# A QKV projection whose start-up is rearranged: one block cut finer, one weight load held back, two products moved forward

## The chip, the cores and the metric

The kernel runs on one core of one Trainium2 chip. Its time is that of one execution on the device in microseconds (us); several executions are taken and their median counts. The core has five engines that each work through their own queue: TensorE (PE, with its weight loads shown apart as PEld), VectorE (DVE), ScalarE (ACT), GpSimd (POOL) and SyncE (SP). In this kernel SP does nothing but issue transfers; ACT and POOL issue a few as well. All transfers of a core share 16 DMA engines.

## The reference, cut to what matters

```
x:     (16, 512, 768)  float32
w_qkv: (768, 2304)     float32

qkv = np.matmul(x, w_qkv)
q, k, v = qkv[..., :768], qkv[..., 768:1536], qkv[..., 1536:]
return np.stack([q, k, v], axis=0).astype(np.float32)
```

It is one product of an 8192 x 768 matrix with a 768 x 2304 matrix, written out as three matrices of 8192 x 768.

## The kernel before, in words

**Tiling.** The 8192 rows are 32 pairs of two 128-row tiles (a pair `p` has rows `r` = 0 and 1). The contraction of 768 is `KT` = 6 slices of 128, in two halves of `KH` = 3 (slices j = 0 to 2 and j = 3 to 5). The 2304 columns are four blocks of 512 (`CB`) in two groups `q` = 0 and 1, each with column blocks `c` = 0 and 1, and 256 remaining columns (`REM`) between the groups.

**Two ways to multiply.** From the third pair (`p` = 2) on, each pair is multiplied with each group `q` by a Strassen-Winograd scheme: a "quad" of 2 x 2 output blocks from seven products of 128 x 384 by 384 x 512 instead of eight (`do(u, 1)` to `do(u, 7)`). Products 1 and 2 take the rounded bf16 rows `xb` and bf16 weights `b1`. The other five take sums of row quarters `sr` (`sums_x`) and sums of weight quarters `ts` (`sum_w`), in f32r. The remaining 256 columns are multiplied plainly in bf16 (`rem`). Pairs 0 and 1 are multiplied wholly in plain bf16 (`block`, `rems_by_halves`), because the sums of the weights do not exist yet while the weights are still arriving.

**The start, where the change lies.** The program's order is written by hand, and each engine keeps that order. SP loads the rows of pairs 0 and 1, then the twelve slices of the weights of group 0 (`load_slices(0, ...)` for column block 0 and `load_slices(1, ...)` for column block 1, one slice j per transfer, the first in two parts), then the rows of pair 2 in eight parts (`load_x_rows(2)`: four for row tile 0, four for row tile 1), then the weights of group 1, column block 0, in two loads (`load_blocks(1, 0)`), and later column block 1 likewise. POOL loads the 256 remaining columns in two K halves, `w_rem[0]` and `w_rem[1]`, 128 x 768 values each, cast to bf16 on the way (L435). It first runs `hold` (L428): a copy of one column that makes POOL wait until a given tile has landed. Before the change it waits once, for slice 5 of column block 0, and issues both halves. A second `hold` waits for the first rows of pair 2; behind it on POOL stands the copy `b22` (L541), one of the operands of product 3.

TensorE's order in that stretch is: block (0, 0) of pairs 0 and 1 (four output tiles, one slice after the other); block (0, 1) of the same tiles; the remaining columns of pairs 0 and 1, first K half for both pairs and then second K half (`rems_by_halves`, L321); products 1 and 2 of pair 2 with group 0 (`do(u, 1)`, `do(u, 2)`); the remaining columns of pair 2 (`rem(2)`, L575); products 5 and 6 (`middle`, L576); then block (1, 0) slice by slice, with products 7, 3 and 4 of pair 2 between its slices (`rest`, `end`).

Block (0, 1) is ordered by groups of slices and tiles: slices 0, 1 and 2 each over all four tiles, and then, tile by tile, slices 3, 4 and 5 together:

```
late = block(
    0, 1, bt, [((j, ), range(4)) for j in range(KH)] + [(range(KH, KT), range(4))]
)
```

A slice of column block 1 must be cast to bf16 (into `bt`) before it is used: slices 0 to 3 on DVE (L450), slices 4 and 5 on ACT (L448). DVE also makes the weight sums (`sum_w`, L120; `sum_w(0, 2)` needs slices 3 to 5 of column block 1) and turns the rows of pair 2 (`transpose(2, 2)`, L154, one instruction for each row tile). ACT rounds the turned rows to bf16, one instruction for each row tile (`round_row`, L200), and copies finished tiles out of the accumulators (`late[n]`, L462; the remaining columns L316; product 1 L253). `do(u, 2)` ends with an addition on DVE that adds product 2 to product 1 (L266).

The accumulators are eight banks used in turn. At this point four belong to block (0, 1), two to the remaining columns of pairs 0 and 1, and two to products 1 and 2 of pair 2. SP's stores of the remaining columns (L317) stand in its queue behind `load_blocks(1, 1)` and ahead of the loads of pair 3 (`load_x_rows(3)`).

Of the kernel before, what the change touches and what calls it, by code (L numbers as in the profile page):

```python
# [10 lines left out]
def kernel(  # L11
# [20 lines left out]
    nc = tc.nc  # L32
# [6 lines left out]
    KT = K // P  # L39
    KH = KT // 2  # L40
    KC = K // 4
    NP = M // (2 * P)
    CB = 512
# [7 lines left out]
    add = mybir.AluOpType.add  # L51
# [34 lines left out]
    bt = both[:, 1].bitcast(bf16).rearrange("p (j n) -> p j n", j=KT)  # L86
# [8 lines left out]
    stage = {}  # L95
# [7 lines left out]
    def load_blocks(q, c):  # L103
        for h in range(2):
            if c == 0 and h == 0:
                t = st_first
            else:
                t = st_pool.tile([P, KH, CB], fp32, name="st1", tag="st")[:]
            load_w(t, h * KH, KH, Q_OFF[q] + c * CB, CB)
            stage[q, h, c] = t  # L110

    def sum_w(q, n):
        t1, t2, t3, t4 = ts[q]
        o, in0, in1 = {
            1: (t1, stage[q, 0, 1], stage[q, 0, 0]),
            2: (t2, stage[q, 1, 1], t1),
            3: (t3, stage[q, 1, 1], stage[q, 0, 1]),
            4: (t4, stage[q, 1, 0], t2),
        }[n]
        nc.vector.tensor_tensor(o, in0, in1, op=sub)  # L120
# [27 lines left out]
    def transpose(p, parts=1):  # L148
        t = xf_pool.tile([P, KT, 2 * P], fp32, name="xf")
        turned = t[:].rearrange("p j (g b) -> p g j b", b=G)  # L150
        rows = xin.pop(p)[:].rearrange("p g (a j) -> p g j a", a=G)
        n = 2 * P // G // parts
        for g in range(0, 2 * P // G, n):
            nc.vector.transpose(turned[:, g:g + n], rows[:, g:g + n])  # L154
        xf[p] = t
# [39 lines left out]
    def round_row(p, r, eng):  # L195
        n = slice(r * P, (r + 1) * P)
        if r == 0:
            xb[p] = xb_pool.tile([P, KT, 2 * P], bf16, name="xb", tag="xb")
        if eng is act:
            eng.activation(xb[p][:, :, n], xf[p][:, :, n], ident)  # L200
        else:
            eng.tensor_copy(out=xb[p][:, :, n], in_=xf[p][:, :, n])
# [23 lines left out]
    def quad(p, q, pool=o_pool, tag="o"):  # L226
        u = Quad()
        u.p, u.q = p, q
        u.o = pool.tile([P, 2, 2 * CB], fp32, name="o", tag=tag)
        u.x = u.y = u.z = None  # L230
        return u

    def product(u, n, ps, start):
        t1, t2, t3, t4 = ts[u.q]
        if n <= 2:
            h = (n - 1) * KH
            lhs = [xb[u.p][:, h + j, :P] for j in range(KH)]
            rhs = [b1[u.q][:, h + j, :] for j in range(KH)]
        else:
            k, t = {3: (4, b22[u.q][:]), 4: (0, t4), 5: (1, t1), 6: (2, t2), 7: (3, t3)}[n]  # L240
            lhs = [sr[u.p][:, k, j, :] for j in range(KH)]
            rhs = [t[:, j, :] for j in range(KH)]
        for j in range(KH):
            nc.tensor.matmul(  # L244
                ps[:], lhs[j], rhs[j],
                start=(start and j == 0), stop=(j == KH - 1), skip_group_check=True,
            )

    def bank():
        return ps_pool.tile([P, CB], fp32, name="ps")  # L250

    def evacuate(u):
        nc.scalar.activation(u.o[:, 0, :CB], u.x[:], ident)  # L253

    def do(u, n, out=True):
        c11, c12 = u.o[:, 0, :CB], u.o[:, 0, CB:]
        c21, c22 = u.o[:, 1, :CB], u.o[:, 1, CB:]
        if n == 1:
            u.x = bank()
            product(u, 1, u.x, True)  # L260
            if out:
                evacuate(u)
        elif n == 2:
            u.z = bank()
            product(u, 2, u.z, True)
            nc.vector.tensor_tensor(c11, c11, u.z[:], op=add)  # L266
        elif n == 6:
            product(u, 6, u.x, False)
            nc.scalar.activation(c12, u.x[:], ident)  # L269
        elif n == 5:  # L270
            u.y = bank()
            product(u, 5, u.y, True)
        elif n == 7:
            product(u, 7, u.x, False)
            nc.scalar.activation(c22, u.x[:], ident)  # L275
            nc.vector.tensor_tensor(c22, c22, u.y[:], op=add)  # L276
        elif n == 4:
            product(u, 4, u.x, False)
            nc.scalar.activation(c21, u.x[:], ident)  # L279
        elif n == 3:  # L280
            product(u, 3, u.y, False)
            nc.vector.tensor_tensor(c12, c12, u.y[:], op=add)  # L282

    def rows_of(s, p, lo, hi):
        return out_flat[s, p * 2 * P:(p + 1) * 2 * P, lo:hi].rearrange("(r m) n -> m r n", m=P)
# [26 lines left out]
    def rem_copied(p, ps, eng=nc.sync):  # L312

        def copied():
            o = or_pool.tile([P, 2, REM], fp32, name="orem")
            act.activation(o[:], ps[:], ident)  # L316
            return lambda: eng.dma_start(rows_of(1, p, R_OFF - H, R_OFF - H + REM), o[:])  # L317

        return copied

    def rems_by_halves(pairs):  # L321
        banks = [ps_pool.tile([P, 2, REM], fp32, name="ps") for _ in pairs]
        for h in range(2):
            for p, ps in zip(pairs, banks):
                for r in range(2):
                    for j in range(KH):
                        nc.tensor.matmul(  # L327
                            ps[:, r, :], xb[p][:, h * KH + j, r * P:(r + 1) * P],
                            w_rem[h][:, j, :], start=(h == 0 and r == 0 and j == 0),
                            stop=(h == 1 and j == KH - 1), skip_group_check=True,  # L330
                        )
        return [rem_copied(p, ps) for p, ps in zip(pairs, banks)]

    def two(a, b, early, u=None):

# [87 lines left out]
    half = CB // 2  # L423
# [4 lines left out]
    def hold(src):  # L428
        mark = m_pool.tile([P, 1], fp32, name="mark")
        nc.gpsimd.tensor_copy(out=mark[:], in_=src)  # L430

    hold(stage[0, 1, 0][:, KH - 1, :1])
    for h in range(2):
        rows = w_qkv.rearrange("(p j) n -> p j n", j=KT)[:, h * KH:(h + 1) * KH]
        nc.gpsimd.dma_start(w_rem[h][:], rows[:, :, R_OFF:R_OFF + REM])  # L435
    hold(xin[2][:, 0, :1])
# [8 lines left out]
    def cast_j(q, c, w, j, eng=act, n=slice(0, CB)):  # L445
        src = stage[q, j // KH, c][:, j % KH, n]
        if eng is act:
            eng.activation(w[:, j, n], src, ident)  # L448
        else:
            eng.tensor_copy(out=w[:, j, n], in_=src)  # L450
# [3 lines left out]
    def block(q, c, w, groups, between={}):  # L454

        ps = {}
        late = []

        def finish(n):
            p, r = divmod(n, 2)  # L460
            u = quads[p, q]
            act.activation(u.o[:, r, c * CB:(c + 1) * CB], ps[n][:], ident)  # L462

        for i, (js, tiles, *cols) in enumerate(groups):
            cols = cols[0] if cols else slice(0, CB)
            for n in tiles:
                p, r = divmod(n, 2)
                fresh = n not in ps
                if fresh:
                    ps[n] = bank()  # L470
                for j in js:
                    nc.tensor.matmul(  # L472
                        ps[n][:, cols], xb[p][:, j, r * P:(r + 1) * P], w[:, j, cols],
                        start=(fresh and j == 0), stop=(j == KT - 1), skip_group_check=True,
                    )
                if KT - 1 not in js:
                    continue
                if (p, q) not in quads:
                    quads[p, q] = quad(p, q)
                late.append(lambda n=n: finish(n))  # L480
            between.get(i, lambda: None)()
        return late
# [51 lines left out]
    for f in late0:  # L534
# [5 lines left out]
    sum_w(0, 2)  # L540
    nc.gpsimd.tensor_copy(out=b22[0][:], in_=stage[0, 1, 1])  # L541
    late = block(
        0, 1, bt, [((j, ), range(4)) for j in range(KH)] + [(range(KH, KT), range(4))]
    )
    rems = rems_by_halves(range(2))
    transpose(2, 2)

    late[0]()
    late[1]()
    round_row(2, 0, act)  # L550
    rem_stores = [rems[0]()]
    late[2]()
    late[3]()
    round_row(2, 1, act)
    rem_stores.append(rems[1]())
    load_blocks(1, 1)
    for store in rem_stores:
        store()
# [7 lines left out]
    sums[2](dve)  # L566
    sum_w(0, 3)
    sums[3](dve)
    sums[4](dve)

    u = quad(2, 0)
    do(u, 1)
    do(u, 2)
    cast_j(1, 0, b1[1], 0)
    rem2 = rem(2)  # L575
    middle(u, (5, 6))  # L576
# [85 lines left out]
```

## Time and profile before

| what | value |
|---|---|
| median of 3 executions | 360.31 us (359.99 to 360.98) |
| profiled execution: its own time | 361.83 us |
| profiled execution: span of its instructions | 360.0 us |
| TensorE busy | 353.4 us, 98% of the span |
| VectorE, ScalarE, GpSimd busy | 227.8, 185.6, 178.6 us |
| granted TensorE clock | 1.00 |
| data moved | 107.73 MB, 299 GB/s over the span |
| transfers of SP's queue; of POOL's queue | 82.4%; 0.8% of 16 engines' span |

The span runs from the first instruction to the last one. The profiled execution's own time lies 1.83 us above its span, and 1.52 us above the median of the executions that were only timed. Times of single instructions below are counted from the start of the span. Matmuls follow each other closely, and each is shown longer than the distance to the next: a 128 x 512 bf16 matmul is shown with 0.38 us, while ten of them in a row take 2.15 us from first start to the next group's start. So the distances between starts, not the busy time, tell how fast TensorE works.

### The profile page before, as it was taken

What the parts mean: (1) busy time and instruction counts of PE and PEld (TensorE: products, weight loads), DVE (VectorE), ACT (ScalarE), POOL (GpSimd) and SP (SyncE); (2) the same over time, 40 slices, a digit from 0 to 9 for tenths busy, and PEclk for the clock granted to TensorE, in tenths of its full rate; (3) what the DMA queues carried; (4) which work ended last, traced back from release to release, by engine and by line L of the source; (5) the groups of instructions that cost most, each with busy time, mean ns of one, the idle gap of its engine ahead of it and who ended that gap; (6) DMA issues with size and microseconds to landing.
All of it is one profiled execution on the core that took longest, in us unless ns stands there. A gap on an engine that the chain in (4) does not pass through costs nothing.

```text
span 360.0 us, 5279 instructions
## 1 busy us (share of the span) xinstructions
PE 353.4 (98%) x1780; PEld 251.2 (70%) x1780; DVE 227.8 (63%) x244; ACT 185.6 (52%) x316; POOL 178.6 (50%) x187
## 2 busy tenths in 40 slices
PE   7999999999999999999999999999999999999995
PEld 3465577777777777777777777777777777777764
DVE  2789776756566675566675566675556676556643
ACT  4469744545454545454545444455444445545443
POOL 0221676446664445664445665444665444665420
PEclk9999999999999999999999999999999999999999
DMA  7998999898998999899999899998999998989767
GB/s 271 330 356 306 332 359 394 257 321 308 275 325 300 296 275 291 280 322 301 291 283 286 284 310 308 292 283 285 288 297 315 293 294 272 296 283 322 292 238 257
DMA packets 82107, 107.73 MB, mean 299 GB/s; under 512 B 5409, under 2 KB 62241, under 8 KB 82081
## 3 DMA queue, kind: packets, MB, share of 16 engines
q1 hardware_dynamic: 66672, 96.35, 82.4%
q10 hardware_dynamic: 14608, 10.65, 8.9%
q0 software_dynamic: 800, 0.39, 0.8%
q8 instruction: 14, 0.23, 0.3%
q14 instruction: 13, 0.10, 0.1%
HBM read 32.28 MB, written 75.50 MB: 299 GB/s over the span
## 4 chain that ended last, share of the span: by engine, by line
PE 93%; DMA 5%; ACT 1%; ACTq 1%; issue 0%
PE ps L244 78%; PE ps L299 11%; PE ps L472 4%; DMA st<-in_w_qkv_dram 3%; DMA touch<-in_x_dram 1%; PE ps L327 1%; ACT o L279 0%; ACTq L370 0%; ACT orem L384 0%; ACT both L448 0%; ACTq L416 0%; ACTq L386 0%; ACTq L384 0%
## 5 line engine op out<-in xcount | busy, mean ns | idle before, releaser
L244 PE MATMUL ps<-t,s 128*128 128x512 f32 x720 | 181.1, 399 | 0.0
L244 PEld LDWEIGHTS ps<-t,s 128*128 128x128 f32 x720 | 134.9, 188 | 30.9 <-ACT o L269 0.3
L191 POOL CAST xb<-xf 128x1536 bf16<-128x1536 f32 x28 | 40.9, 1462 | 131.1 <-DVE xf L154 131.1
L276 DVE TENSOR_TENSOR o<-o,ps 128x512 f32<-128x512 f32 x58 | 39.9, 687 | 90.5 <-ACT o L275 90.5
L154 DVE STREAM_TRANSPOSE xf<-xin 128x1536 f32<-128x1536 f32 (+1 forms) x32 | 88.9, 2783 | 2.6 <-DMA xin<-in_x_dram 2.5
L244 PE MATMUL ps<-b,xb 128*128 128x512 bf16 x360 | 87.7, 380 | 0.0
L244 PEld LDWEIGHTS <-xb 128*128 128x128 bf16 x360 | 32.8, 98 | 37.3 <-issue 7.6
L269 ACT ACTIVATE o<-ps 128x512 f32<-128x512 f32 x60 | 35.9, 598 | 44.0 <-PE ps L244 41.3
L275 ACT ACTIVATE o<-ps 128x512 f32<-128x512 f32 x58 | 34.7, 598 | 44.3 <-PE ps L244 44.3
L282 DVE TENSOR_TENSOR o<-o,ps 128x512 f32<-128x512 f32 x60 | 41.2, 687 | 21.4 <-PE ps L244 20.2
L244 PE MATMUL ps<-b,s 128*128 128x512 f32 x180 | 50.4, 389 | 0.0
L253 ACT ACTIVATE o<-ps 128x512 f32<-128x512 f32 x60 | 35.8, 597 | 24.4 <-DVE o L282 20.6
L279 ACT ACTIVATE o<-ps 128x512 f32<-128x512 f32 x60 | 35.9, 598 | 24.2 <-PE ps L244 21.3
L299 PE MATMUL ps<-w_rem,xb 128*128 128x256 bf16 x360 | 44.6, 273 | 0.0
L299 PEld LDWEIGHTS <-xb 128*128 128x128 bf16 x360 | 34.9, 98 | 11.1 <-issue 1.1
L266 DVE TENSOR_TENSOR o<-o,ps 128x512 f32<-128x512 f32 x60 | 37.8, 670 | 2.0 <-ACT o L253 1.3
L244 PEld LDWEIGHTS ps<-b,s 128*128 128x128 f32 x180 | 33.8, 188 | 7.1
L212 POOL TENSOR_TENSOR s<-s,xf 128x384 fp32r<-128x384 f32 x29 | 29.4, 1014 | 2.3
L215 POOL TENSOR_TENSOR s<-xf,s 128x384 fp32r<-128x384 f32 x29 | 29.4, 1015 | 0.0
L213 POOL TENSOR_TENSOR s<-xf 128x384 fp32r<-128x384 f32 x29 | 29.4, 1013 | 0.0
L211 POOL TENSOR_TENSOR s<-xf 128x384 fp32r<-128x384 f32 x29 | 29.3, 1012 | 0.0
L316 ACT ACTIVATE orem<-ps 128x512 f32<-128x512 f32 x31 | 18.5, 597 | 20.6 <-PE ps L299 20.1
(47 smaller groups left out, 125.9 us busy)
## 6 DMA issues: line engine op xcount, KB each, us to landing
out_dram<-o SPq DMA_DIRECT2D x62, 768.0 KB, 4.9
out_dram<-o SPq DMA_DIRECT2D x65, 256.0 KB, 4.0
xin<-in_x_dram SPq DMA_DIRECT2D x62, 192.0 KB, 6.9
xin<-in_x_dram ACTq DMA_DIRECT2D x50, 192.0 KB, 4.3
out_dram<-orem SPq DMA_DIRECT2D x31, 256.0 KB, 5.9
st<-in_w_qkv_dram SPq DMA_DIRECT2D x11, 256.0 KB, 5.8
st<-in_w_qkv_dram SPq DMA_DIRECT2D x3, 768.0 KB, 8.7
xin<-in_x_dram SPq DMA_DIRECT2D x4, 384.0 KB, 5.1
```

Source lines behind the costliest of these rows:

```text
L154: nc.vector.transpose(turned[:, g:g + n], rows[:, g:g + n])
L191: nc.gpsimd.tensor_copy(out=xb[p][:], in_=xf[p][:])
L212: 2: lambda g: g.tensor_tensor(s[:, 2], s[:, 1], a11, op=sub),
L244: nc.tensor.matmul(ps[:], lhs[j], rhs[j], start=(start and j == 0), stop=(j == KH - 1), skip_group_check=True,)
L253: nc.scalar.activation(u.o[:, 0, :CB], u.x[:], ident)
L266: nc.vector.tensor_tensor(c11, c11, u.z[:], op=add)
L269: nc.scalar.activation(c12, u.x[:], ident)
L275: nc.scalar.activation(c22, u.x[:], ident)
L276: nc.vector.tensor_tensor(c22, c22, u.y[:], op=add)
L279: nc.scalar.activation(c21, u.x[:], ident)
L282: nc.vector.tensor_tensor(c12, c12, u.y[:], op=add)
L299: nc.tensor.matmul(ps, xb[p][:, j, r * P:(r + 1) * P], w_rem[j // KH][:, j % KH, :], start=(j == 0), stop=(j == KT - 1), skip_group_check= ...
```

## The change

Three things are rearranged; the number of matmuls, transfers and additions stays the same.

- **Block (0, 1) is cut further.** Slices 0 to 3 (not 0 to 2) go over all four tiles one after the other, and only slices 4 and 5 go together, tile by tile.
- **The second half of the remaining columns' weights is held back.** `hold` is called before each of the two loads: for slice 5 of column block 0 before `w_rem[0]`, and for slice 5 of column block 1 before `w_rem[1]`. On POOL's queue the second `hold` and the second load now stand ahead of the `hold` on pair 2's rows and the `b22` copy.
- **Products 1 and 2 of pair 2 go between the two K halves of the remaining columns.** `rems_by_halves` now issues the first K half and returns a function for the second one. TensorE's order becomes: block (0, 1), first half, products 1 and 2, second half, `rem(2)`. ACT's order becomes: tiles 0 and 1 of the block, row tile 0 of pair 2 rounded, tiles 2 and 3, product 1 copied out, row tile 1 rounded, then the remaining columns of pairs 0 and 1. The addition of product 2 is split off (`add_z`) and placed on DVE between `sums[3]` and `sums[4]` of pair 2.

```
--- before.py
+++ after.py
+    def add_z(u):
+        c11 = u.o[:, 0, :CB]
+        nc.vector.tensor_tensor(c11, c11, u.z[:], op=add)
+
...
             product(u, 2, u.z, True)
-            nc.vector.tensor_tensor(c11, c11, u.z[:], op=add)
+            if out:
+                add_z(u)
...
     def rems_by_halves(pairs):
         banks = [ps_pool.tile([P, 2, REM], fp32, name="ps") for _ in pairs]
-        for h in range(2):
+
+        def half(h):
             for p, ps in zip(pairs, banks):
                 for r in range(2):
                     for j in range(KH):
...
-        return [rem_copied(p, ps) for p, ps in zip(pairs, banks)]
+
+        half(0)
+        return lambda: half(1), [rem_copied(p, ps) for p, ps in zip(pairs, banks)]
...
-    hold(stage[0, 1, 0][:, KH - 1, :1])
     for h in range(2):
+        hold(stage[0, 1, h][:, KH - 1, :1])
         rows = w_qkv.rearrange("(p j) n -> p j n", j=KT)[:, h * KH:(h + 1) * KH]
         nc.gpsimd.dma_start(w_rem[h][:], rows[:, :, R_OFF:R_OFF + REM])
     hold(xin[2][:, 0, :1])
...
     late = block(
-        0, 1, bt, [((j, ), range(4)) for j in range(KH)] + [(range(KH, KT), range(4))]
+        0, 1, bt,
+        [((j, ), range(4)) for j in range(KH + 1)] + [(range(KH + 1, KT), range(4))],
     )
-    rems = rems_by_halves(range(2))
+    second_half, rems = rems_by_halves(range(2))
     transpose(2, 2)
 
     late[0]()
     late[1]()
     round_row(2, 0, act)
-    rem_stores = [rems[0]()]
     late[2]()
     late[3]()
+    u = quad(2, 0)
+    do(u, 1)
+    do(u, 2, False)
     round_row(2, 1, act)
-    rem_stores.append(rems[1]())
+    second_half()
+    rem_stores = [r() for r in rems]
     load_blocks(1, 1)
     for store in rem_stores:
         store()
...
     sum_w(0, 3)
     sums[3](dve)
+    add_z(u)
     sums[4](dve)
 
-    u = quad(2, 0)
-    do(u, 1)
-    do(u, 2)
     cast_j(1, 0, b1[1], 0)
     rem2 = rem(2)
```

## The prediction

> **What bounds the kernel now.** I read first the chain of waits that ended last, for the first 30 us, then the waits of TensorE, and then the four engines in order of time around the one place the chain names.
>
> ```profile
> 11.43 6.25 DMA st<-in_w_qkv_dram
> 17.68 0.02 issue
> 17.70 0.64 ACT both L448
> 18.34 0.04 issue
> 18.39 2.32 PE ps L472 x10
> ...
> PE ps L472 <- ACT both L448: 0.2, 1, 0.2
> ```
>
> The last weight slice lands at 17.68, ACT casts it, and from 18.39 TensorE's groups join end to end. The last line is the only wait of TensorE from 18 us to the end. So TensorE is the bound: a wait removed before 18.39 is won whole, and a wait inserted behind it is paid whole. TensorE's order of time sizes what can be won:
>
> ```profile
> 14.97 3.19 PE L472 MATMUL ps<-both,xb 128*128 128x512 bf16 x14
> 18.39 2.32 PE L472 MATMUL ps<-both,xb 128*128 128x512 bf16 x10 [0.23 <-ACT both L448]
> 20.54 2.78 PE L327 MATMUL ps<-w_rem,xb 128*128 128x256 bf16 x24
> 23.16 1.46 PE L244 MATMUL ps<-b,xb 128*128 128x512 bf16 x6
> 24.46 1.47 PE L299 MATMUL ps<-w_rem,xb 128*128 128x256 bf16 x12
> ```
>
> Paces from first start to next start: (20.54 - 18.39)/10 = 0.215 us for 512 columns, (23.16 - 20.54)/24 = 0.109 for 256, (24.46 - 23.16)/6 = 0.217 for products 1 and 2. The first 14 matmuls would end at 14.97 + 14 x 0.215 = 17.98; the 15th starts at 18.39. The hole is **0.41 us**, and nothing else in this stretch can be won.
>
> What the moved work needs stands in the order of time of DVE, ACT and POOL (one after the other here), and in the view of the remaining columns' weights (last line):
>
> ```profile
> 16.73 0.42 DVE L450 CAST both<-st 128x512 bf16<-128x512 f32 x1
> 17.81 1.76 DVE L120 TENSOR_TENSOR t<-st,t 128x1536 fp32r<-128x1536 f32 x1 [0.66 <-DMA st<-in_w_qkv_dram]
> 19.66 1.60 DVE L154 STREAM_TRANSPOSE xf<-xin 128x768 f32<-128x768 f32 x1
> 22.53 1.58 DVE L154 STREAM_TRANSPOSE xf<-xin 128x768 f32<-128x768 f32 x1 [1.28 <-DMA xin<-in_x_dram]
> ...
> 21.29 0.84 ACT L200 ACTIVATE xb<-xf 128x768 bf16<-128x768 f32 x1 [1.25 <-DVE xf L154]
> ...
> 12.80 0.44 POOL L430 COPY mark<-st 128x1 f32<-128x1 f32 x1 [11.49 <-DMA st<-in_w_qkv_dram]
> 13.18 1.69 POOL L435 DMA_DIRECT2D w_rem<-in_w_qkv_dram  x2
> 19.68 0.18 POOL L430 COPY mark<-xin 128x1 f32<-128x1 f32 x1 [4.81 <-DMA xin<-in_x_dram]
> ...
> 39.03 3.87 POOL L202 CAST xb<-xf 128x768 bf16<-128x768 f32 x1 [6.49 <-DVE xf L154]
> DMA to landing us min/median/max: 6.5/7.0/7.6
> ```
>
> Row tile 0 of pair 2 is turned at 21.26 and rounded at 21.29 + 0.84 = 22.13. POOL issues the two halves at 13.18 and 14.10, and they land 6.5 and 7.6 us after their issue, at 19.7 and 21.7; TensorE reads them from 20.54 and 21.85.
>
> **The change part by part.** Every duration is of the profiled execution (span 360.0, own time 361.83); the shift found is then set on the median of 360.31, 1.52 lower.
>
> *Finer block.* Slice 5 is first read by the 18th matmul instead of the 15th: 14.97 + 17 x 0.215 = 18.63, and ACT's cast ends at 17.70 + 0.63 = 18.33. Slice 3 is wanted at 14.97 + 12 x 0.215 = 17.55 (DVE done at 17.15), slice 4 at 18.41 (ACT done at 17.26). The hole closes: **-0.41**. The cover is 0.3 us; if the last slice landed later than by that, the wait would come back.
>
> *The held load: what it frees.* Of the 800 packets of POOL's transfers, 407 had started by 17.7, and the first half landed at 19.7, behind the last slice (17.68). A slice therefore shares its engines with the first half whether or not the second stands behind it. I take 0 for an earlier slice; the other end is 0.66, DVE's idle time ahead of `sum_w`. The second row tile of pair 2 may land up to 1.28 earlier (DVE's wait at 22.53, to 21.26), but that is on no path of TensorE's.
>
> *The held load: when it arrives.* The mark can start at about 17.7 (ACT starts 0.02 after the landing), and the issue follows 0.13 to 0.38 behind (19.68 to 19.81, POOL's next instruction after the second mark, and 12.80 to 13.18): 17.85 to 18.1. Landing then is bounded by 4.3 us (x loads issued by ACT, the quickest comparable median) and 7.6 us: 22.15 to 25.7. I take 6.5, the row of the half that had no other transfer of POOL's queue ahead: 17.86 + 6.5 = **24.36**. Its company will be the 768 KB loads of `load_blocks(1, 0)`, issued from 18.05, so I see no reason for less. The Trainium skill would put it far earlier: DMA: Bandwidth & Descriptors, Anatomy of one DMA — SWDGE (gpsimd) path, fits 2.0 us plus bytes over 436e3 per us, an estimate of 2.45 us for 192 KB, a landing at 20.3 and no wait at all; the two transfers here took 6.5 and 7.6 beside a full SP queue, so I do not follow it.
>
> *Products 1 and 2 moved.* TensorE now ends the block at 14.97 + 24 x 0.215 = 20.13 and the first K half (12 x 0.109) at 21.44. Products 1 and 2 want row tile 0 rounded, 22.13: the 12 matmuls of the second half, which hid the turning and rounding, no longer stand ahead. TensorE waits 0.7. The rounding does not come sooner, as it hangs on the turning (19.66), on `sum_w(0, 2)` ahead of it on DVE, and on the 17.68 landing. Products end at 22.15 + 6 x 0.217 = 23.45. The second half would then end at 24.76 against 24.46 before: **+0.30 net, with the 0.41 already counted**. With the landing at 24.36 it starts at 24.40 and ends at 25.71: **+1.25**, of which 0.95 is the wait for the held load.
>
> *ACT.* Product 1 is copied out (0.61) ahead of row tile 1's rounding: ACT is free of tiles 2 and 3 at 22.13 + 1.08 = 23.2, copies until 23.7, and rounds by 25.0 at latest. `rem(2)` wants that at 25.71 + 0.65 = 26.4. Both copies of the remaining columns now stand behind the second half, at 25.2 and 26.0, so the cast of slice 0 for block (1, 0) ends at 27.2 instead of 26.5; the block wants it at 27.17 + 1.25 = 28.4. Cost 0.
>
> *SP.* The two stores of the remaining columns wait for those copies (second at 26.6, before 25.52). Queued behind are pair 3's loads (from 27.1, before 26.0), whose rows DVE turned at 35.86, after the last part's landing at 34.3; one later is still in time. The stores of pairs 0 and 1 behind them gate nothing on TensorE. Cost 0.
>
> *DVE and POOL.* The addition (0.68) goes ahead of `sums[4]`, which ends at 28.76 instead of 28.16; product 3 read it at 28.82 and now comes 1.25 later. Cost 0, but without a later TensorE the cover would be 0.06. The `b22` copy (19.81 before, 1.47) has until 28.8 too. The 768 KB load read by ACT at 25.85 landed at 23.9; the displaced half costs it at most its half of 0.8% of the span, 1.4 us, so 25.3; ACT comes to it at 26.6. Cost 0.
>
> *Sum:* -0.41 + 0.71 + 0.95 = +1.25, carried to the end because TensorE never waits afterwards: 361.83 + 1.25 = 363.1 profiled, 360.31 + 1.2 = **361.5** as median.
>
> **The rivals.** Each shift is landing + 0.04 + 1.31 - 24.46, and at least +0.30 unless the rounding moves too.
>
> *A, the forecast:* landing between 23.6 and 25.7, shift +0.5 to +2.6.
>
> *B, the load is hidden after all:* it lands before 23.45, that is within 5.6 us of its issue. For it: the loads of pair 2's rows landed in 4.6 to 6.4 us at the same time, and only one transfer is issued, not two. Against: the two rows of its own kind. Shift +0.30: 360.6.
>
> *C, DVE shuts POOL out of the mark.* The mark and `sum_w(0, 2)` are released by the same landing. Where the two ran together one stood still: the cast at 39.03 took 3.87 and ended 0.7 after the second of two DVE sums had (42.21), though POOL's casts of twice the size have a mean of 1462 ns; the mark at 12.80 took 0.44 and ended with a DVE cast, the one at 19.68, beside a turning, 0.18. If DVE is first, the mark ends with the sum at 19.6, the issue comes at 19.7 and the landing at 26.2: +3.1, 363.4. It decides when the mark starts after DVE's 17.81; I expect 17.7 to 17.75, just ahead. In the Trainium skill, SBUF — State Buffer, Who interferes with whom, says the same: a DVE instruction with two SBUF inputs and a GpSimd one that reads SBUF exclude each other for the whole instruction, and the first to issue wins. The 3.87 agrees with it.
>
> *D, not slower:* the freed transfers bring the last slice 0.66 earlier, with it `sum_w`, the turning and the rounding (21.47, when TensorE is free), and the held load too, by 22.75. Then the whole 0.41 is won: 359.9. Against: the first half is ahead of the second in POOL's queue and outlasts the slice; and product 3 would wait for `sums[4]` unless pair 2's second rows come earlier as well.
>
> **How the numbers follow.** A 0.53, B 0.17, C 0.21, D 0.06, and 0.03 for a gain that I cannot name. About 0.3% (1.08 us) is what a measurement of this kernel can tell from no change. Slower by more than that needs a landing after 24.2: two thirds of A (0.35) and all of C: 0.56. Within it: the rest of A (0.18), B and D, 0.41. Faster by over 0.3%: the unnamed 0.03, as no part of the change shows more than 0.41 to win. The time is A's, 361.5. The range goes from 360.0, which leaves out D (359.9), to 363.4, which leaves out C's upper half: 0.8 or a little more.
>
> **What would show it.** TensorE: no gap near 18.4, a wait of about 0.7 on ACT's rounding near 21.5, and one of about 1 on the transfer ahead of the second half (new inner function, L334 to L337). POOL: second mark near 17.7, its length against DVE's sum telling A from C; the held half's landing 6 to 7 us after its issue. Wrong if that landing stands before 23.45, if the last slice lands well before 17.68, or if TensorE shows waits after 26 us that I costed at nothing.

## The result, and the profile after

The changed kernel takes 363.63 us (median of 6 executions, 363.06 to 366.19) against 360.29 for the kernel before: a ratio of 1.0094, 95% interval 1.0074 to 1.0114. It is 3.3 us slower. The forecast was slower, 361.5, with a range that ended at 363.4: the sign was right, the size was not.

The profiled execution of the changed kernel took 363.42 us, with a span of 361.6. The chain of waits of its first 30 us no longer goes from the last weight slice by ACT's cast to TensorE. It goes from that slice to POOL's mark and through the held load:

```profile
10.38 6.11 DMA st<-in_w_qkv_dram
16.49 0.06 issue
16.54 0.12 POOL mark L438
16.66 8.03 DMA w_rem<-in_w_qkv_dram
24.69 0.04 issue
24.73 1.47 PE ps L333 x12
26.20 1.31 PE ps L304 x12
```

The columns are start, length and what it is (the step that ended last). The load is issued at 16.66, 0.17 us after the last slice has landed, and lands 8.03 us later. Then the waits of TensorE, and its order of time (start, busy time, group, and in brackets the idle time ahead with what ended it):

```profile
PE ps L333 <- DMA w_rem<-in_w_qkv_dram: 2.1, 1, 2.1
PE ps L244 <- ACT xb L200: 0.6, 1, 0.6
```

```profile
13.92 5.34 PE L480 MATMUL ps<-both,xb 128*128 128x512 bf16 x24
19.10 1.47 PE L333 MATMUL ps<-w_rem,xb 128*128 128x256 bf16 x12
21.17 1.47 PE L244 MATMUL ps<-b,xb 128*128 128x512 bf16 x5 [0.60 <-ACT xb L200]
24.73 1.47 PE L333 MATMUL ps<-w_rem,xb 128*128 128x256 bf16 x12 [2.09 <-DMA w_rem<-in_w_qkv_dram]
26.04 1.47 PE L304 MATMUL ps<-w_rem,xb 128*128 128x256 bf16 x12
27.27 1.64 PE L244 MATMUL ps<-t,s 128*128 128x512 f32 x6
```

The block's 24 matmuls stand in one group without a hole: the finer cut did what it was to do. Behind it are two new waits, before products 1 and 2 (21.17) and before the second K half (24.73).

The two profiles cannot be laid over each other by their own clocks, because block (0, 1) starts at 14.97 in the first profile of the kernel before and at 13.92 here, though the work ahead of it is the same in both programs. In all profiles of this study it starts between 13.6 and 15.0, with no order among the kernels. It follows the landing of the last rows of pairs 0 and 1, which the trace reports in 16 parts. In the first profile of the kernel before, the last part comes at 8.79, 1.0 us after the other fifteen; in the first profile of the changed kernel it comes at 7.75, 0.1 us after the others. What can be compared is the stretch from the start of block (0, 1) to the first f32 matmul (product 5 of pair 2): 25.68 - 14.97 = 10.71 before, 27.27 - 13.92 = 13.35 after, **+2.64**. From that matmul to the end of the span it is 334.4 in both (360.05 - 25.68 and 361.63 - 27.27). Everything that the change does to the profiled time happens in those 13 us, and nothing is given back or lost later. The medians lie 3.3 us apart; where the rest lies is taken up below.

### The profile page after: what moved, and what is told of

Same layout as the page of the kernel before. It is cut to its first block, busy times and chain, and to the rows that moved or that the text cites. A ratio compares the mean times of both kernels' runs of the same rounds, so it can differ in the third digit from the quotient of the medians.

```text
span 361.6 us, 5247 instructions
## 1 busy us (share of the span) xinstructions
PE 350.5 (97%) x1748; PEld 250.8 (69%) x1780; DVE 227.7 (63%) x244; ACT 185.7 (51%) x316; POOL 178.5 (49%) x188
## 4 chain that ended last, share of the span: by engine, by line
PE 91%; DMA 6%; issue 1%; ACT 1%; ACTq 1%; POOL 0%
PE ps L244 77%; PE ps L304 11%; DMA st<-in_w_qkv_dram 3%; PE ps L480 3%; DMA w_rem<-in_w_qkv_dram 2%; DMA touch<-in_x_dram 1%; PE ps L333 0%; ACT o L284 0%; ACTq L378 0%; ACT orem L392 0%; ACTq L424 0%; ACTq L394 0%; POOL mark L438 0%; ACTq L392 0%
## 5 line engine op out<-in xcount | busy, mean ns | idle before, releaser
L244 PE MATMUL ps<-b,xb 128*128 128x512 bf16 x330 | 81.4, 379 | 2.6 <-ACT xb L200 0.6
L253 ACT ACTIVATE o<-ps 128x512 f32<-128x512 f32 x60 | 35.8, 597 | 24.4 <-DVE o L287 20.7
L211 POOL TENSOR_TENSOR s<-xf 128x384 fp32r<-128x384 f32 x29 | 30.8, 1062 | 0.0
L321 ACT ACTIVATE orem<-ps 128x512 f32<-128x512 f32 x31 | 18.5, 597 | 22.2 <-PE ps L304 19.9
L213 POOL TENSOR_TENSOR s<-xf 128x384 fp32r<-128x384 f32 x29 | 29.4, 1014 | 0.0
```

Source lines behind the costliest of these rows:

```text
L211: 1: lambda g: g.tensor_tensor(s[:, 1], a21, a22, op=add),
L244: nc.tensor.matmul(ps[:], lhs[j], rhs[j], start=(start and j == 0), stop=(j == KH - 1), skip_group_check=True,)
```

## The experiments

The theory was: the held half landed late because it shares the DMA engines with the 768 KB loads of `load_blocks(1, 0)`, which in the kernel before had hardly begun to move when it was transferred ("company"). The rival: a transfer of POOL's queue takes about 8 us in this stretch whatever else runs ("fixed"). Below, "stretch" is always from block (0, 1) to product 5.

| kernel | ratio to before (95%) | stretch, us | held half: issue to landing, us |
|---|---|---|---|
| before (two profiles) | 1 | 10.71, 10.83 | not held: 7.6, 7.6 |
| changed (two profiles) | 1.0094 (1.0074 to 1.0114), 1.0102 (1.0075 to 1.0129) | 13.35, 13.72 | 8.0, 8.3 |
| changed without the hold | 1.0006 (0.9997 to 1.0014) | 11.17 | not held: 7.7 |
| changed, big loads wait | 1.0035 (1.0023 to 1.0047) | 11.28 | 4.9 |
| changed, hold 3 slices earlier | 1.0015 (1.0006 to 1.0024) | 10.99 | 6.1 |
| hold alone | 1.0142 (1.0123 to 1.0160) | 14.59 | 7.9 |
| before, long hold | 1.0303 (1.0286 to 1.0319) | 21.80 | 6.6 |
| finer block alone | 1.0000 (0.9991 to 1.0008) | 10.75 | not held: 7.4 |
| finer block, hold 3 slices earlier (two profiles) | 0.9997 (0.9988 to 1.0006), 0.9995 (0.9983 to 1.0006) | 10.33, 10.94 | 6.1, 7.0 |

**The changed kernel without the hold.**

```
-    for h in range(2):
-        hold(stage[0, 1, h][:, KH - 1, :1])
+    hold(stage[0, 1, 0][:, KH - 1, :1])
+    for h in range(2):
```

> The changed kernel with both halves of the remaining columns' weights issued at the old place; finer block and moved products stay. Both theories of the held load (company: it took 8.03 us because it shares the engines with the 768 KB loads; fixed: a transfer of POOL's queue in this stretch takes about 8 us whatever else runs) expect no wait at the second K half, as the second half landed at 21.7 before: what is left is the 0.41 us won by the finer block and the 0.71 us wait of products 1 and 2 for the rounded rows, +0.3 us, 360.6. If the products' move costs more than that wait, it shows here as 361 or more.

Measured: 360.87 us beside 360.66, +0.2. The wait at the second K half is gone from TensorE's waits, and the one for the rounded rows (0.7) is left, as expected. So taking the hold out of the changed kernel takes 1.0094 - 1.0006, about 0.9% or 3.1 us, away; the finer block and the moved products together cost almost nothing.

**The finer block alone** (the new groups of block (0, 1) in the kernel before).

> The kernel before with the finer block alone. Both theories: the 0.41 us hole ahead of the last slices closes and TensorE never waits afterwards, so 359.9 (-0.4 us, 0.1%). If the gain is given back to a later wait, 360.3.

Measured: no difference, and the stretch is 10.75. The hole did close, but the 0.4 us went into a wait that the kernel before hardly has. The waits of TensorE, and the order of time around it:

```profile
PE ps L299 <- ACT xb L200: 0.2, 1, 0.2
```

```profile
14.11 5.34 PE L472 MATMUL ps<-both,xb 128*128 128x512 bf16 x24
19.29 2.82 PE L327 MATMUL ps<-w_rem,xb 128*128 128x256 bf16 x24
21.95 1.46 PE L244 MATMUL ps<-b,xb 128*128 128x512 bf16 x5
23.25 0.82 PE L299 MATMUL ps<-w_rem,xb 128*128 128x256 bf16 x6
24.27 0.83 PE L299 MATMUL ps<-w_rem,xb 128*128 128x256 bf16 x6 [0.21 <-ACT xb L200]
```

```profile
21.75 1.58 DVE L154 STREAM_TRANSPOSE xf<-xin 128x768 f32<-128x768 f32 x1 [0.97 <-DMA xin<-in_x_dram]
```

`rem(2)` comes 0.4 us sooner and stands before the rounding of pair 2's second row tile, which hangs on the turning, which waits for its rows. Six 256-column matmuls take 6 x 0.109 = 0.65, so from 23.25 the next six could start at 23.90; they start at 24.27. This is the next bound behind the last slice, 0.4 us away. In the first profile of the kernel before, the hole hides it: the rounding ends at 24.15 + 0.85 = 25.00 and is wanted at 24.46 + 0.65 = 25.11.

**The changed kernel, with the big loads waiting for the held half.**

```
     hold(xin[2][:, 0, :1])
+    nc.gpsimd.tensor_copy(out=st_first[:, 0, :1], in_=w_rem[1][:, KH - 1, :1])
     load_blocks(1, 0)
```

> The changed kernel, but the two 768 KB loads of group 1, column block 0, wait until the held half has landed. Company theory: landing falls from 8.03 us after the issue to about 5.0 (first packet 3.0 after the issue as in both profiles, 25 packets per engine at 60 ns, and half a us to land), which is before products 1 and 2 end; the 2.1 us wait at the second K half goes, 361.5 us if the later big loads bring no wait of their own, up to 363 if the casts for block (1, 0) become late. Fixed theory: landing still 8 us after the issue, the wait of 2.1 us stays, 363.6 or more.

Measured: the half lands 4.9 us after its issue (17.03 to 21.89), where the fixed theory said 8. TensorE's wait for it is gone, and the ratio to before falls from 1.0094 to 1.0035. Company is shown. The DMA queues say how. First the changed kernel, two windows that together hold its 400 packets (18.2 to 21.2 and 21.2 to 24.5; per queue: packets, MB, share of 16 engines):

```profile
q1 hardware_dynamic: 508, 0.83, 89.3%
q0 software_dynamic: 110, 0.06, 13.6%
...
q1 hardware_dynamic: 514, 1.01, 81.5%
q0 software_dynamic: 290, 0.14, 32.2%
```

Then the kernel with the big loads waiting (18.5 to 21.6), and the kernel before (15.4 to 21.2, both halves):

```profile
q0 software_dynamic: 400, 0.20, 54.6%
q1 hardware_dynamic: 106, 0.07, 7.1%
```

```profile
q1 hardware_dynamic: 1186, 1.08, 67.4%
q0 software_dynamic: 799, 0.39, 50.4%
```

In the changed kernel the first of the half's packets starts at 19.9, 3.2 us after the issue. From there to 24.5, while POOL's queue (q0) moves the 400 packets, SP's queue (q1) moves 1.37 MB (1.84 MB in both windows). In the kernel before it moves 1.08 MB while POOL's queue moves twice as many. The half is not slower by itself. It lost its place beside small row loads and got one beside 768 KB loads.

With the big loads waiting, the first packet starts 1.5 us after the issue instead of 3.2, and the packets are spread over 3.0 us instead of 4.5. So about half of the 3.2 us gained lies ahead of the first packet. The expectation had 3.0 and 1.5 us for these two parts: that its sum of 5.0 was met is luck. The late start does not need the big loads: in the changed kernel the first half's packets, too, start 3.0 us after its issue (12.12 to 15.15), before any big load is issued. This experiment takes away nearly all other traffic; that small row loads cost less than big ones rests on the next one, where the last 400 of POOL's packets start within 2.2 us, and on the kernel before. What it is in the big loads, their size or the number that waits, no run separates.

The time is still 1.2 us above the kernel before. Of that the profile shows 0.5 in the stretch (the wait for the rounded rows, 0.78) and 0.1 after it, where ACT now waits 1.4 us for the delayed big load. The rest is not in the profiled execution's stretch; where it lies stays open.

**The changed kernel, held for slice 2 of column block 1 instead of slice 5.**

```
-        hold(stage[0, 1, h][:, KH - 1, :1])
+        hold(stage[0, 1 - h, h][:, KH - 1, :1])
```

> The changed kernel with the second half's load held for slice 2 of column block 1 instead of slice 5, some 2.9 us earlier. Company theory: beside the small row loads it lands as before, 6.5 to 7.6 us after its issue. Fixed theory: 8.0 us after its issue. Either way it lands before products 1 and 2 end, so the wait at the second K half goes and the time is that of the kernel without the hold, 360.6. If the last slice of column block 1 lands later than with the late hold by more than 0.3 us, the finer block's cover is gone and it is 0.2 to 0.6 us more.

Measured: +0.4 us (0.2 of it in the stretch), and no wait for the load is left in TensorE's list. It lands 6.1 us after its issue: a little under the lower end of what company gave, and not 8. The half is quick again where it comes before the big loads move. The last slice did not suffer: it lands 2.65 us after the start of the block, against 2.57 and 2.70 in the changed kernel.

**The hold alone, in the kernel before.**

> The kernel before with the hold on the second half alone: no finer block, products at their old place. Company theory: the second K half follows the first at once, so TensorE waits for the whole of the late landing: the half lands 8.0 us after its issue at 2.6 us behind the start of the block's 14th matmul, about 10.8 us after block (0, 1) starts, where TensorE wants it 6.9 after: a wait of 3.9 us, 364.3. Products 1 and 2 then hide 1.3 us of it in the changed kernel, against the 0.4 us that it wins by the finer block. Fixed theory gives the same here; a landing at the earlier rate of 6.5 us after the issue would give 362.8.

Measured: 365.97 us, +5.1 by the ratio's middle. TensorE waits 3.8 us for the load, as computed, and the stretch is 14.59, +3.8. The time misses the expectation by 1.7 us, and three of the four executions had a mean granted clock of 0.994 or 0.989; the one at 1.0 took 365.27, which is still 1.0 above the expectation. That led to the experiment with a long hold, below.

**Both kernels a second time.**

> The changed kernel a second time, for its profile and a narrower interval. The stretch from the start of block (0, 1) to product 5 was 13.35 us against 10.71 before, +2.64, while the medians lie 3.34 apart. Company theory: the stretch comes out again between 13 and 14 us with the held half 8 us or more after its issue, and the medians 2.6 to 3.4 apart. If the stretch is again near 13.35 and the medians are still over 3 apart, 0.5 us or so lies ahead of block (0, 1) or in the profile of before not being a typical execution, and the second profile of the kernel before tells which.

> The kernel before a second time, for its profile. In the first one block (0, 1) starts at 14.97, about 1 us later than in the five other profiles (13.6 to 14.2), and its span is 1.2 us over what the timed executions suggest. Expected here: block (0, 1) at 13.6 to 14.2, the stretch to product 5 10.4 to 10.8, and from product 5 to the end 334.4 as everywhere.

Measured: the changed kernel 364.04 us, stretch 13.72, the half 8.3 us after its issue. The kernel before: block (0, 1) at 14.16, stretch 10.83, 334.4 from there to the end. So the stretch grows by 2.5 to 3.0 us (four pairs of profiles), and the medians lie 3.3 apart in both timings. The executions of the changed kernel at a mean clock of 0.999 or more have medians of 363.54 and 363.80, which is 3.1 to 3.25 above before. So 0.3 to 0.8 us of the slowdown lie outside the stretch and are not placed. The profiled execution of the kernel before is no typical one (1.5 us above the median in the first profile, 0.4 in the second), while those of the changed kernel lie within 0.3 us of theirs.

**A long hold: what the wait does to the clock** (the kernel before, with the second half held until the first 768 KB load has landed).

```
-    hold(stage[0, 1, 0][:, KH - 1, :1])
+    load_blocks(1, 0)
     for h in range(2):
+        hold([stage[0, 1, 0], stage[1, 0, 0]][h][:, KH - 1, :1])
...
-    load_blocks(1, 0)
```

> The kernel before with the second half held until the first 768 KB load of group 1 has landed, so that TensorE waits some 9 to 11 us at the second K half instead of 0 (kernel before), 2.1 to 2.3 (changed kernel) or 3.8 (hold alone). It asks about the granted clock. In the changed kernel 3 of 12 executions so far had a mean clock of 0.995 and were 2.4 to 2.9 us longer than the others; with the wait of 3.8 us 3 of 4 were at 0.994 or less; in the kernel before none of 45 was under 0.998. Theory 1: a wait that is long enough lowers the clock for a while afterwards, and 2 us is on the edge: here every execution is at 0.996 or less, and the profile shows the clock below 1 behind the wait; about 371 to 374 us. Theory 2: the lower clock has nothing to do with the wait: most executions are at 0.998 to 1.0 here.

Measured: 371.88 us, mean clocks of 0.984 to 0.991 in all four executions. Theory 1 holds for a wait of 9 us; that 2 us is on the edge, this run cannot show. TensorE ends its last matmul at 20.7 and starts again at 29.7. By stretches (length, then busy time and instructions of PE, PEld, DVE, ACT and POOL, granted clock, DMA share, GB/s):

```profile
23.00:24.00 1.00, 0.00 (x0) 0.00 (x0) 1.00 (x2) 0.00 (x0) 1.00 (x3) 1.00 1.06 412
24.00:24.50 0.50, 0.00 (x0) 0.00 (x0) 0.50 (x1) 0.00 (x0) 0.50 (x1) 0.79 1.07 414
24.50:25.00 0.50, 0.00 (x0) 0.00 (x0) 0.50 (x2) 0.00 (x0) 0.50 (x2) 0.50 1.03 397
...
31.00:33.00 2.00, 1.83 (x8) 1.09 (x8) 0.00 (x0) 1.84 (x4) 0.00 (x0) 0.50 0.15 54
33.00:35.00 2.00, 1.95 (x8) 0.91 (x8) 0.08 (x1) 1.95 (x4) 0.00 (x0) 0.62 0.27 94
35.00:37.00 2.00, 2.00 (x16) 1.73 (x14) 2.00 (x2) 0.00 (x0) 0.00 (x0) 1.00 0.95 256
```

The clock halves at 24.3 (which gives the mean of 0.79 from 24.0 to 24.5), some 3.6 us after the last matmul. It stays there until about 34.5 (which gives the 0.62 from 33 to 35), 4.8 us after the matmuls have come back: the 12 of the second K half take 32.20 - 29.68 = 2.5 us instead of 1.3, and products 1 and 2 behind them 34.65 - 32.20 = 2.45 instead of 1.3. The held half, issued when the row loads and the first big load have landed, has only 0.21 MB of SP's queue beside its packets and lands 6.6 us after its issue, not 8.

**The finer block with the early hold, products at their old place.** This was the version that the runs pointed to: the rows of pair 2 come sooner, so the finer block's gain should not be taken back.

> The finer block with the products at their old place, and the second half held for slice 2 of column block 1. The finer block alone won nothing in time: its 0.41 us went into a wait of TensorE for the rounding of pair 2's second row tile, whose rows had landed 7.45 us after the block's start, behind both halves of the remaining columns. With the early hold those rows landed 6.83 after it. Company theory: the half lands about 6.4 after the block's start, TensorE wants it at 6.5, the rows come 0.6 earlier, both waits are gone: 0.3 to 0.4 us faster than before. If the held half is late here by some tenths, it is the same as before.

> The finer block with the early hold and the products at their old place, a second time, for the interval. The profiled stretch from block (0, 1) to product 5 was 10.33 us against 10.71 and 10.83 in the two profiles of the kernel before, so 0.4 to 0.5 us faster is expected if the profile is typical; the first timing gave 0.03% faster with an interval from 0.12% faster to 0.06% slower. Rival: the start of block (0, 1) comes a little later with the other order of the loads and takes the gain back; then no difference again.

Measured: 0.9997 and 0.9995. The first profile shows no wait at all and a stretch of 10.33; the second shows 10.94. There the first half lands late, at 19.79, where TensorE could have started at 14.40 + 24 x 0.215 = 19.56, and the held half at 21.46, with a wait of TensorE's of 0.2 us. Both halves land just when they are wanted, sometimes later, and the 0.3 to 0.5 us that were expected do not show in the time. No version was found that measurably beats the kernel before.

## Why the prediction was wrong

- **The bound, and that a wait behind it is paid whole: right.** From product 5 on every profile takes 334.3 to 334.5 us.
- **Finer block, -0.41: right in the changed kernel** (no hole in the 24 matmuls). That it is a gain of its own was not right: alone it is worth nothing, as above.
- **An earlier last slice, taken as 0: right.** The last one lands 2.57 and 2.70 us after the start of block (0, 1) in the two profiles of the changed kernel, 2.71 and 2.63 in those of the kernel before. In the first profiles the last two slices come 1.01 and 1.21 us apart (14.27, 15.28, 16.49 in the changed kernel) against 1.13 and 1.07 before (15.48, 16.61, 17.68). At that time POOL's queue is moving the first half in both kernels.
- **Products 1 and 2 waiting 0.7 for the rounding: right.** The first half's twelve matmuls start at 19.10 and take 1.31, so the wait is 21.17 - 20.41 = 0.76. Without the hold it is what is left.
- **The issue of the held load, 2.9 us after the block's start: right** (2.74 and 2.87). Rival C, the mark blocked by DVE's sum, did not happen in either profile of the changed kernel. In order of time, POOL and then DVE (first profile):

```profile
16.54 0.18 POOL L438 COPY mark<-st 128x1 f32<-128x1 f32 x1 [3.51 <-DMA st<-in_w_qkv_dram]
16.66 0.79 POOL L443 DMA_DIRECT2D w_rem<-in_w_qkv_dram  x1
...
16.61 1.76 DVE L120 TENSOR_TENSOR t<-st,t 128x1536 fp32r<-128x1536 f32 x1 [0.57 <-DMA st<-in_w_qkv_dram]
```

  The mark came 0.07 us ahead of the sum and took 0.18. The time near C's 363.4 is therefore not C's doing.
- **The landing, 6.5 us after the issue: the step that failed.** It took 8.0 and 8.3, above even the upper bound of 7.6. The bound came from two transfers that had moved beside small row loads. The prediction named the 768 KB loads as company and concluded only that there was "no reason for less", where it should have asked what more they cost. It landed 10.77 us after the start of block (0, 1), which on the prediction's clock is 25.74, the very end of rival A's range. With 8.0 the wait before the second K half is 24.73 - (21.17 + 1.30) = 2.26 instead of 0.95, and the sum becomes -0.41 + 0.76 + 2.26 = +2.6, the measured growth of the stretch. Set on the median of 360.31, that gives 362.9. The last 0.7 us to 363.63 is not in this term and stays open; with the second pair of profiles (+3.0) it is 0.3. The page of the Trainium skill that was weighed there, DMA: Bandwidth & Descriptors, Anatomy of one DMA — SWDGE (gpsimd) path, would have given an estimate of 2.45 us; even with hardly anything beside it the half took 4.9 here.
- **ACT, SP, DVE and POOL at nothing: right**, by the unchanged 334.4.
- **Not foreseen:** executions with a lower mean clock, three of twelve, told at the end. They are too few to set the median.

## What to carry to other kernels

A load that is held back is not the same load later: ask what will be moving when it finally goes, and take its duration from a transfer in that company, or count the other queue's bytes per packet of its own. Before filling a hole on the bounding engine, look for the wait that stands just behind it, since it may be hidden by the hole itself and take the gain. Where executions differ in their start, compare the profiles from a common event, not from time zero.

## What the runs showed of the hardware that was not expected

A wait of TensorE can cost more than its length. In the long hold it waits 9.0 us, and the matmuls behind it then run at half clock and take 2.4 us more than elsewhere (2.5 and 2.45 us instead of 1.3 each; 0.2 of it is a gap between them).

Whether waits of 2 to 4 us do the same is argued, not shown. Of the 12 timed executions of the changed kernel three had a mean granted clock of 0.995, and they took 366.0 to 366.8 us against 363.1 to 364.1 for the others. With the hold alone, 3.8 us of wait in the profile, three of four were at 0.994 or less; with 9 us all were. Of the 62 executions of the kernel before that were timed beside the experiments none lay under 0.998. A mean of 0.995 over 362 us is about what 3.6 us at half clock would give (0.5 x 3.6 / 362 = 0.005). That is at most 1.8 us of matmul time, and these executions are 2.2 to 3.0 us longer than the median of the others, so the clock alone does not make the difference. No profiled execution caught the lower clock in these kernels, so how long TensorE waited there is not known. A later landing of the held half, with a longer wait, could be behind both the time and the clock; this rival was not tested.

The Trainium skill, TensorE: Matmul & The Clock Gate, Part 1: The HAM clock gate, says that the clock halves after an idle window of about 3.4 us and returns after a busy one, with windows that run freely. The 3.6 us in the long hold agrees. If the executions at 0.995 waited no longer than the profiled 2.1 to 2.3 us, that would be shorter than the page leads one to expect.
